# Stacked queries and keys of the first head: transfers issued ahead of the spatial gating, with the weights' priority

## The chip, the cores and the metric

The kernel runs on one core of one Trainium2 chip. The metric is device time in microseconds (us), one launch for the whole computation. The time before is 2175.99 us, the median of three runs (2171.11, 2175.99, 2178.37).

## The reference, cut to what matters

The program is one hybrid layer (dilated attention beside a gated linear recurrence, width 1024, 512 tokens) followed by two layers of a second kind on the same 512 tokens, which also read a context of 256 tokens. The change lies in the second kind alone. One such layer, shortened:

```
zc = split(modulate(rms(h_ctx)) @ w_in[l], 10)      # 256 context tokens
zx = split(modulate(rms(x)) @ w_in[l], 10)          # 512 tokens
k1, k2 = concat(context keys, token keys)           # 768 keys for the tokens
y_a = conformer_conv(a_val, a_gate)                 # 31 taps
p1 = softmax(q1 k1^T * s); p2 = softmax(q2 k2^T * s)
y_b = rms((p1 - lam * p2) @ v)                      # 4 heads, 32 + 32 wide queries, 64 wide values
y_c = gelu(u) * (w_s @ layer_norm(gelu(v)))         # spatial gating
y_d = bg * depthwise_conv(cg * xin)                 # short convolution
x = x + gate * concat(y_a, y_b, y_c, y_d) @ w_out
x = x + gate2 * relu(modulate(rms(x)) @ w1)^2 @ w2
if l == 0: the same mixer and channel mixer on the context, which attends to its own 256 keys
```

## The kernel before, in words

Everything is held transposed, channels on the 128 partitions and tokens along the row. Every float32 operand of a matmul is kept as a rounded high part and a low part (`split`, L188), and a product is three matmuls (`mm3`, L156: high by high L157, high weights by low activations L158, low weights by high activations L159; `tok3` L164 to L166 for outputs that have tokens on the partitions).

**Weights.** A weight block comes as two halves of 128x1024. `raw_half` (L132) issues one 512 KB transfer on SyncE's queue (SP) into the tile `raw`, which has four buffers, under a priority raised by `HP` = 4000. `whalf` (L144) casts it to `whi` on ScalarE (L149) and takes the rest, `wlo`, on VectorE (L150); that last step frees the raw buffer, and the next transfer waits for it. `whi` and `wlo` have three buffers each.

**Order.** The code is traced in program order and a scheduler draws up the order of each engine's instructions ahead of the run: of the instructions that are ready by its own reckoning it takes the one of the best priority, which is the place in program order, moved forward under `tc.high_priority(offset=HP)` and back under `bg(...)`. On the chip each engine, and SP's queue of transfers too, then goes through its list strictly in that order, and an instruction that has to wait holds up what stands behind it.

**The mixer.** `Mixer` holds one stream: the context `sc` (256 tokens, layer 0 only, `mc`) or the tokens `sx` (`mx`). Its parts are `conv` (gated input, then 31 taps on VectorE, L872, most of them in the background), `qkv`, `spatial`, `short`, `attention`, `conv_norm` and `out_part`. The sequence is: `mc.conv`, `mc.qkv`, `mc.spatial`, `mc.short`, `mc.attention`; then per layer `mx.conv`, `mx.qkv`, in layer 0 `mc.conv_norm` and `mc.out_part` (with the context rows `xc` read back from memory, L1215, and stored, L1217), then `mx.spatial` and `mx.attention`, within which `short` and `out_part` of the tokens are run in the background.

**Stacking.** `qkv` leaves queries and keys as [128, 2, n] tiles (two heads of 2 x 32 channels on the partitions, high and low part). For the scores, `load_head` copies each head's 32 rows into a [96, 2, n] tile three times, queries as high, low, high (`qst`) and keys as high, high, low (`kst`), so that one matmul over 96 rows makes the three products of `mm3`. These are transfers from SBUF to SBUF on SP (L1034), 32 partitions each: per head of the context 6 of queries and 6 of keys, per head of the tokens 6 of queries and 12 of keys (two key sources). Both tiles have `ST_BUFS` = 2 buffers, so two heads are in flight. The pool `stk` that they come from opens after `hc`, which holds the rotary table `rope`, is closed, and before the pools of the spatial gating.

**Attention.** One unit is a head and 128 queries: scores `sc` (L1057), maximum (L1061), exponentials (L1065), the difference of the two softmaxes, transposes (L1081), the product with v (L1084). The scores of the next unit are traced ahead of the current unit's rest. For the tokens the scores take three banks of PSUM in the pool `ps_d`, which is opened after the pool that the spatial gating used is closed, so they lie on banks that the gating has to leave first (its last reader there is L951 on VectorE, `sb`).

Of the kernel before, what the change touches and what calls it, by code (L numbers as in the profile page):

```python
# [10 lines left out]
F32 = mybir.dt.float32  # L11
F32R = mybir.dt.float32r
# [67 lines left out]
def tile_net(ctx: ExitStack, tc: tile.TileContext, wst, vec, crow, lrow, sgw, cst, xT, xN, cT, out):  # L80
    nc = tc.nc
    V, A, G, T = nc.vector, nc.scalar, nc.gpsimd, nc.tensor
    HP = 4000
    uid = [0]

    def nm(s):
        uid[0] += 1
        return f"{s}_{uid[0]}"

    def open_pool(name, side="left", space=None, bufs=1):  # L90
        kw = {} if space is None else {"space": space}
        g = tc.tile_pool(name=name, bufs=bufs, side=side, reuse_waits="tile", **kw)
        return g, g.__enter__()
# [104 lines left out]
    class Sums:  # L198


        def __init__(self, n, acc=None, bank=None):
            self.n, self.acc, self.bank, self.parts = n, acc, bank or (lambda: ps.mm()), [] if acc is None else [acc]
# [185 lines left out]
    for mp in range(4):  # L388
        u = yap.tile([P, 2, SX], F32, tag="ya", name=nm("u"), bufs=4)
        for i in range(2):  # L390
            m = 2 * mp + i
            dst, src = u[:, i].rearrange("p (i r) -> p r i", r=4), pu[m].rearrange("p (r i) -> p r i", r=4)
# [297 lines left out]
    sx, sc = S(), S()  # L690
# [117 lines left out]
    class Mixer:  # L808


        def __init__(self, l, s, kv, mix, y_tile):
            self.l, self.s, self.kv, self.mix, self.y_tile = l, s, kv, mix, y_tile
            self.y = {}

        def tt(self, name, full=False):
            t = self.mix.tile([P, self.s.n + 4], F32, tag="t", name=nm(name), bufs=TA_BUFS)
# [196 lines left out]
                self.y["a", m] = a  # L1013


        def attention(self, k, bp, stp_, keys, between):
            s = self.s
            nkeys = sum(q.n for q in keys)
            kts = [(q, i) for q in keys for i in range(q.nt)]
            nk = len(kts)  # L1020
            ng = 2 * s.nt

            class Head:
                pass

            def load_head(h):
                hd = Head()
                hd.h = h
                hd.q = stp_.tile([96, 2, s.n], F32R, tag="qst", name=nm("qst"), bufs=ST_BUFS)
                hd.k = stp_.tile([96, 2, nkeys], F32R, tag="kst", name=nm("kst"), bufs=ST_BUFS)  # L1030

                def stack(dst, src, blk, rows):
                    for i, hl in enumerate(rows):
                        nc.sync.dma_start(dst[32 * i:32 * i + 32].bitcast(F32),  # L1034
                                          src[32 * blk:32 * blk + 32, hl].bitcast(F32))

                for w in range(2):
                    blk = 2 * (h % 2) + w
                    stack(hd.q[:, w], s.q[h // 2], blk, (0, 1, 0))
                    o = 0  # L1040
                    for q in keys:
                        stack(hd.k[:, w, o:o + q.n], q.k[h // 2], blk, (0, 0, 1))
                        o += q.n
                return hd

            def weights(hd, qt):

                sm = const.tile([P, 8], F32, tag="sm2", name=nm("sm"), bufs=8)
                if nkeys > 512:
                    st = ps.tile([P, 3, 512], F32, "sc3", nm("sc3")).rearrange("p a b -> p (a b)")  # L1050
                else:
                    st = ps.mm("sc")
                for w in range(2):
                    o = w * nkeys
                    while o < (w + 1) * nkeys:
                        e = min((w + 1) * nkeys, (o // 512 + 1) * 512)
                        T.matmul(st[:, o:e], hd.q[:, w, qt * P:(qt + 1) * P], hd.k[:, w, o - w * nkeys:e - w * nkeys],  # L1057
                                 start=True, stop=True, skip_group_check=True)
                        o = e
                s3 = st[:, :2 * nkeys].rearrange("p (w k) -> p w k", w=2)  # L1060
                V.tensor_reduce(sm[:, 0:2], s3, axis=AX.X, op=ALU.max, negate=True)  # L1061
                pw = []
                for w in range(2):
                    p = bp.tile([P, nkeys], F32, tag=f"p{w}", name=nm("p"), bufs=P_BUFS)
                    A.activation(p, s3[:, w], AF.Exp, bias=sm[:, w:w + 1], accum_out=sm[:, 4 + w:5 + w])  # L1065
                    pw.append(p)
                return pw, sm

            def apply(hd, qt, pw, sm):

                h = hd.h
                V.reciprocal(sm[:, 6:7], sm[:, 5:6])
                V.scalar_tensor_tensor(sm[:, 7:8], sm[:, 6:7], sm[:, 4:5], k.nlam, op0=ALU.mult, op1=ALU.mult)
                V.scalar_tensor_tensor(pw[0], pw[1], sm[:, 7:8], pw[0], op0=ALU.mult, op1=ALU.add)
                V.reciprocal(hd.r1[:, qt, h % 2:h % 2 + 1], sm[:, 4:5])
                pth = bp.tile([P, nkeys], F32, tag="pth", name=nm("pth"), bufs=PT_BUFS)
                for t0 in range(0, nkeys, 512):
                    tn = min(512, nkeys - t0)
                    pt = ps.mm()
                    for i in range(tn // P):  # L1080
                        T.transpose(pt[:, i * P:(i + 1) * P], pw[0][:, t0 + i * P:t0 + (i + 1) * P], ident)  # L1081
                    A.copy(pth[:, t0:t0 + tn], pt[:, :tn])
                for i, (ss, kt) in enumerate(kts):
                    T.matmul(hd.po[:, qt, h % 2], pth[:, i * P:(i + 1) * P], ss.v[:, kt, h],  # L1084
                             start=i == 0 and qt == 0 and h % 2 == 0, stop=i == nk - 1 and qt == s.nt - 1 and h % 2 == 1,
                             skip_group_check=True)

            def heads_norm(o, r1):

                of = o.rearrange("p t h d -> p (t h) d")  # L1090
                rf = r1.rearrange("p t h -> p (t h)")
                sq = bp.tile([P, ng, 64], F32, tag="osq", name=nm("osq"), bufs=1)
                A.activation(sq, of, AF.Square)
                ms = const.tile([P, 16], F32, tag="ms", name=nm("ms"), bufs=3)
                m2 = const.tile([P, 16], F32, tag="ms2", name=nm("ms2"), bufs=2)
                V.tensor_reduce(ms[:, :ng], sq, axis=AX.X, op=ALU.add)
                V.tensor_mul(m2[:, :ng], rf, rf)
                V.tensor_mul(ms[:, :ng], ms[:, :ng], m2[:, :ng])
                V.tensor_scalar(ms[:, :ng], ms[:, :ng], 1.0 / 64.0, EPS, op0=ALU.mult, op1=ALU.add)
                rs = rstd_small(ms[:, :ng], ng)  # L1100
                V.tensor_mul(m2[:, :ng], rs[:, :ng], rf)
                V.tensor_mul(sq, of, m2[:, :ng].unsqueeze(2).broadcast_to([P, ng, 64]))
                pq = ps.mm()
                s2 = sq.rearrange("p (t h) d -> p t (h d)", h=2)
                for i in range(s.nt):
                    T.transpose(pq[:, i * P:(i + 1) * P], s2[:, i], ident)
                a = self.y_tile("b")
                split(a, pq[:, :s.n], k.subg)
                self.y["b", len([q for q in self.y if q[0] == "b"])] = a

            heads = {0: load_head(0)}
            units = [(h, qt) for h in range(4) for qt in range(s.nt)]
            nxt = weights(heads[0], 0)
            for un, (h, qt) in enumerate(units):
                hd = heads[h]
                if qt == 0:
                    if h < 3:
                        heads[h + 1] = load_head(h + 1)
                    if h % 2 == 0:
                        po = ps.mm("po")[:, :ng * 64].rearrange("p (t h d) -> p t h d", h=2, d=64)  # L1120
                        r1 = const.tile([P, s.nt, 2], F32, tag="r1", name=nm("r1"), bufs=2)
                    hd.r1 = r1
                    hd.po = po
                cur = nxt
                if un + 1 < len(units):
                    h2, qt2 = units[un + 1]
                    nxt = weights(heads[h2], qt2)
                apply(hd, qt, *cur)
                if un in between:
                    between[un]()  # L1130
                if self.taps[0] < 31:
                    self.conv_taps(k, self.taps[0] + CONV_STEP)
                if qt == s.nt - 1 and h % 2:
                    heads_norm(po, r1)
# [8 lines left out]
        def out_part(self, names, done=None, bank=None):  # L1143
# [3 lines left out]
            for half in range(2):  # L1147
                w = {n: whalf((key, 2 + half), "ab".index(n), 512) for n in names if n in "ab"}
                for pair in range(2):
                    if "c" in names:  # L1150
                        w["cd"] = whalf((key, half), pair, 256)
                    for i in range(2):
# [7 lines left out]
                        for e, ((hi, lo), kk, mi, a) in enumerate(seq):  # L1160
# [8 lines left out]
                                                         name=nm("y"), bufs=4 if name in "cd" else 8))  # L1169
# [19 lines left out]
    for l in range(2):  # L1189
# [9 lines left out]
        mx = Mixer(l, sx, [sx] if l == 0 else [sx, sc], mix, y_tile)  # L1199
# [20 lines left out]
        g_st, stk = open_pool("stk")  # L1220
        g_y, yp = open_pool("yp", side="right")
        g_s, sgp = open_pool("sgp", side="right")
        mx.spatial(kx, sgp)
        close_pool(g_s)
        ps.close()
# [120 lines left out]
ST_BUFS = 2  # L1346
# [158 lines left out]
```

## Time and profile before

| | |
|---|---|
| median of three runs | 2175.99 us |
| profiled execution | 2175.18 us, span 2173.3 us |
| TensorE busy | 94% of the span, 11020 matmuls |
| VectorE, ScalarE, GpSimd busy | 66%, 37%, 1% |
| DMA | 37.6% of 16 engines, 259.47 MB, 119 GB/s |
| mean granted TensorE clock | 0.978 of full |

The profile is one execution. Its span is the time from the first to the last instruction seen by the profiler; the 1.9 us between it and the execution's own time lie around it. A busy TensorE is not one at its peak, since the ends of matmuls are modelled. "Idle before, releaser" names the event that came last before an instruction began; "issue" there means that the profile shows no event for it.

### The profile page before, as it was taken

The numbers are of one execution on the slowest core, as the hardware profiler recorded it, in microseconds if no ns is written. First come the engines' busy times: TensorE is split into PE (matmuls) and PEld (weight loads), VectorE is DVE, ScalarE is ACT, GpSimd is POOL, SyncE is SP. The second block draws the span as 40 slices with busy tenths as digits, with TensorE's granted clock in tenths as the row PEclk, the third lists the DMA queues.
The fourth block names the chain that finished last, engine by engine and source line by source line (L and its number), as shares of the span: only waits on it lengthen the run. The fifth ranks groups of instructions, "written<-read, shape, count | busy, mean of one in ns | idle before, by whom it ended". The sixth has DMA issues, their size and how long they took to land.

```text
span 2173.3 us, 28000 instructions
## 1 busy us (share of the span) xinstructions
PE 2053.4 (94%) x11020; PEld 1758.3 (81%) x11020; DVE 1424.4 (66%) x2351; ACT 810.1 (37%) x1266; POOL 27.4 (1%) x28
## 2 busy tenths in 40 slices
PE   7989999999999988998999999999998998999997
PEld 5778788778889777876888888888887787888886
DVE  8778999843458999778354645534798766443444
ACT  3565333432344533645312313123434544232331
POOL 0000000000000000000000000000000000000000
PEclk9999999999999999998999999999999998999998
DMA  8523666523335444222232454422413212333331
GB/s 314 171 92 95 197 222 204 181 94 105 109 111 168 124 121 127 78 78 79 67 127 88 138 169 150 155 67 89 135 59 107 83 59 69 97 97 97 97 97 58
DMA packets 84388, 259.47 MB, mean 119 GB/s; under 512 B 11424, under 2 KB 20256, under 8 KB 84256
## 3 DMA queue, kind: packets, MB, share of 16 engines
q1 hardware_dynamic: 84256, 257.67, 37.6%
q8 instruction: 87, 1.43, 0.3%
q14 instruction: 45, 0.37, 0.1%
HBM read 242.95 MB, written 5.24 MB: 114 GB/s over the span
## 4 chain that ended last, share of the span: by engine, by line
PE 72%; DVE 18%; DMA 3%; issue 3%; ACT 3%; POOL 1%; SPq 0%; POOLq 0%; DVEq 0%; ACTq 0%
PE mm L157 15%; PE mm L159 15%; PE mm L158 15%; PE g L157 5%; PE g L158 5%; PE g L159 5%; DVE wlo L150 3%; DVE ya L872 2%; PE po L1084 2%; DVE rawa L263 2%; DVE j L263 1%; PE sc L1057 1%; DMA rawa<-wst 1%; PE mm L1081 1%; PE mm L208 1%
## 5 line engine op out<-in xcount | busy, mean ns | idle before, releaser
L149 ACT CAST whi<-raw 128x1024 fp32r<-128x1024 f32 x312 | 326.9, 1050 | 536.7 <-PE mm L158 387.4
L150 DVE TENSOR_TENSOR wlo<-raw,whi 128x1024 fp32r<-128x1024 f32 x312 | 380.5, 1222 | 210.7 <-ACT whi L149 205.9
L157 PE MATMUL mm<-h,whi 128*128 128x512 f32 (+1 forms) x992 | 361.0, 366 | 5.7 <-ACT h L338 3.6
L158 PE MATMUL mm<-h,whi 128*128 128x512 f32 (+1 forms) x992 | 361.7, 365 | 0.9 <-DVE h L712 0.9
L159 PE MATMUL mm<-h,wlo 128*128 128x512 f32 (+1 forms) x992 | 361.1, 364 | 0.8 <-DVE wlo L150 0.8
L159 PE MATMUL mm<-hid,wlo 128*128 128x512 f32 (+1 forms) x768 | 272.6, 355 | 1.0 <-DVE wlo L150 1.0
L157 PE MATMUL mm<-hid,whi 128*128 128x512 f32 (+1 forms) x768 | 273.0, 355 | 0.0
L158 PE MATMUL mm<-hid,whi 128*128 128x512 f32 (+1 forms) x768 | 272.8, 355 | 0.0
L157 PEld LDWEIGHTS mm<-h,whi 128*128 128x128 f32 x992 | 188.8, 191 | 37.1 <-ACT h L338 4.0
L158 PEld LDWEIGHTS mm<-h,whi 128*128 128x128 f32 x992 | 188.7, 190 | 31.5 <-DVE h L712 1.9
L157 PE MATMUL g<-h,whi 128*128 128x512 f32 x512 | 205.7, 402 | 8.6 <-DVE v L508 6.0
L159 PEld LDWEIGHTS mm<-h,wlo 128*128 128x128 f32 x992 | 188.6, 190 | 31.2 <-DVE wlo L150 2.0
L158 PE MATMUL g<-h,whi 128*128 128x512 f32 x512 | 204.8, 400 | 0.0
L159 PE MATMUL g<-h,wlo 128*128 128x512 f32 x512 | 204.3, 399 | 0.3 <-DVE wlo L150 0.3
L159 PEld LDWEIGHTS mm<-hid,wlo 128*128 128x128 f32 x768 | 146.1, 190 | 21.5 <-DVE wlo L150 1.4
L157 PEld LDWEIGHTS mm<-hid,whi 128*128 128x128 f32 x768 | 146.4, 191 | 20.2
L158 PEld LDWEIGHTS mm<-hid,whi 128*128 128x128 f32 x768 | 146.3, 191 | 20.0
L1284 DVE SCALAR_TENSOR_TENSOR r<-mm,r 128x512 f32<-128x512 f32 x96 | 57.4, 599 | 114.1 <-ACT r L1283 114.0
L157 PEld LDWEIGHTS g<-h,whi 128*128 128x128 f32 x512 | 98.4, 192 | 26.9 <-issue 6.2
L159 PEld LDWEIGHTS g<-h,wlo 128*128 128x128 f32 x512 | 98.1, 192 | 19.3 <-DVE wlo L150 0.7
L158 PEld LDWEIGHTS g<-h,whi 128*128 128x128 f32 x512 | 98.3, 192 | 17.9
L872 DVE SCALAR_TENSOR_TENSOR ya<-glu,caw,ya 128x512 f32<-128x512 f32 (+1 forms) x180 | 111.6, 656 | 0.5
(309 smaller groups left out, 3462.7 us busy)
## 6 DMA issues: line engine op xcount, KB each, us to landing
raw<-wst SPq DMA_DIRECT2D x312, 512.0 KB, 3.9
rawa<-wst SPq DMA_DIRECT2D x120, 512.0 KB, 4.6
qst<-q SPq DMA_DIRECT2D x48, 64.0 KB, 2.0
kst<-k SPq DMA_DIRECT2D x48, 64.0 KB, 2.0
kst<-k SPq DMA_DIRECT2D x72, 32.0 KB, 2.1
x<-xT SPq DMA_DIRECT2D x4, 512.0 KB, 5.0
hs_d<-c SPq DMA_DIRECT2D x4, 512.0 KB, 2.6
hq<-hs_d SPq DMA_DIRECT2D x4, 512.0 KB, 5.5
```

Of the source, the lines that this page charges most:

```text
L149: A.copy(hi, src)
L150: V.tensor_sub(lo, src, hi.bitcast(F32))
L157: T.matmul(ps, lh, rh, start=start, stop=False)
L158: T.matmul(ps, lh, rl, start=False, stop=False)
L159: T.matmul(ps, ll, rh, start=False, stop=stop)
L208: T.matmul(pt[:, i:i + 1], a[:, i * P:(i + 1) * P], ones1, start=k == 0 and i == 0, stop=k == len(self.parts) - 1 and i == nt - 1, skip_gr ...
L263: V.tensor_tensor_reduce(o, w, row, 0.5, 0.0, ALU.mult, ALU.add, d)
L872: V.scalar_tensor_tensor(self.ya[m], x, w, self.ya[m], op0=ALU.mult, op1=ALU.add)
L1057: T.matmul(st[:, o:e], hd.q[:, w, qt * P:(qt + 1) * P], hd.k[:, w, o - w * nkeys:e - w * nkeys], start=True, stop=True, skip_group_check=True)
L1081: T.transpose(pt[:, i * P:(i + 1) * P], pw[0][:, t0 + i * P:t0 + (i + 1) * P], ident)
L1084: T.matmul(hd.po[:, qt, h % 2], pth[:, i * P:(i + 1) * P], ss.v[:, kt, h], start=i == 0 and qt == 0 and h % 2 == 0, stop=i == nk - 1 and q ...
L1284: V.scalar_tensor_tensor(r, p, 0.0, r, op0=ALU.max, op1=ALU.mult)
```

## The change

`load_head` becomes a method of `Mixer`, without changes to the tiles that it allocates. Three things differ. In the token mixers of both layers, head 0 is loaded right after the pools are opened and before `spatial` is traced, and `attention` takes that head from `mx.first` (the context mixer has none and loads head 0 in `attention` as before). Every transfer of every head of all three attentions is issued under the priority that weights have (`HP`). And within a head the keys go first, then the queries.

```
@@ class Mixer
-            self.y = {}
+            self.y, self.first = {}, None
...
+        def load_head(self, h, stp_, keys):
+            s, hd = self.s, S()
+            hd.h = h
+            hd.q = stp_.tile([96, 2, s.n], F32R, tag="qst", name=nm("qst"), bufs=ST_BUFS)
+            hd.k = stp_.tile([96, 2, sum(q.n for q in keys)], F32R, tag="kst", name=nm("kst"), bufs=ST_BUFS)
+
+            def stack(dst, src, blk, rows):
+                for i, hl in enumerate(rows):
+                    with tc.high_priority(offset=HP):
+                        nc.sync.dma_start(dst[32 * i:32 * i + 32].bitcast(F32),
+                                          src[32 * blk:32 * blk + 32, hl].bitcast(F32))
+
+            for w in range(2):
+                blk, o = 2 * (h % 2) + w, 0
+                for q in keys:
+                    stack(hd.k[:, w, o:o + q.n], q.k[h // 2], blk, (0, 0, 1))
+                    o += q.n
+                stack(hd.q[:, w], s.q[h // 2], blk, (0, 1, 0))
+            return hd
@@ attention
-                        nc.sync.dma_start(dst[32 * i:32 * i + 32].bitcast(F32),
-                                          src[32 * blk:32 * blk + 32, hl].bitcast(F32))
-                for w in range(2):
-                    blk = 2 * (h % 2) + w
-                    stack(hd.q[:, w], s.q[h // 2], blk, (0, 1, 0))
-                    o = 0
-                    for q in keys:
-                        stack(hd.k[:, w, o:o + q.n], q.k[h // 2], blk, (0, 0, 1))
-                        o += q.n
...
-            heads = {0: load_head(0)}
+            heads = {0: self.first or self.load_head(0, stp_, keys)}
...
-                        heads[h + 1] = load_head(h + 1)
+                        heads[h + 1] = self.load_head(h + 1, stp_, keys)
@@ layers
         g_s, sgp = open_pool("sgp", side="right")
+        mx.first = mx.load_head(0, stk, [sx, sc])
         mx.spatial(kx, sgp)
```

## Rows read from the trace of the kernel before

**Rows 1.** The page: engine busy us; DMA issues with KB each, us to landing.

```profile
PE 2053.4 (94%) x11020; PEld 1758.3 (81%) x11020; DVE 1424.4 (66%) x2351; ACT 810.1 (37%) x1266; POOL 27.4 (1%) x28
...
raw<-wst SPq DMA_DIRECT2D x312, 512.0 KB, 3.9
...
kst<-k SPq DMA_DIRECT2D x48, 64.0 KB, 2.0
```

**Rows 2.** Stretches: length, then busy PE, PEld, DVE, ACT, POOL, PEclk, DMA, GB/s.

```profile
700.00:760.00 60.00, 56.20 (x347) 48.46 (x347) 53.99 (x138) 30.41 (x70) 1.80 (x2) 0.99 0.45 132
...
842.00:860.00 18.00, 13.12 (x64) 10.60 (x64) 17.24 (x35) 6.85 (x10) 1.39 (x2) 0.94 0.04 15
860.00:920.00 60.00, 60.00 (x342) 50.37 (x341) 46.78 (x75) 35.43 (x70) 1.01 (x1) 0.96 0.33 95
...
1656.00:1662.00 6.00, 0.64 (x4) 0.47 (x3) 5.89 (x10) 1.36 (x3) 0.00 (x0) 0.83 0.29 76
1662.00:1667.00 5.00, 5.00 (x14) 3.96 (x14) 4.88 (x9) 0.70 (x2) 0.00 (x0) 0.52 0.68 185
```

**Rows 3.** TensorE's waits, 685 to 770 us: total, times, longest.

```profile
PE sc L1057 <- DMA kst<-k: 3.1, 2, 2.1
```

**Rows 4.** Context attention, SP, DVE, ACT in time: start, duration, engine, what.

```profile
702.90 1.86 SPq L1034 DMA_DIRECT2D qst<-q  x3
...
707.43 1.20 DVE L150 TENSOR_TENSOR wlo<-raw,whi 128x1024 fp32r<-128x1024 f32 x1
...
708.67 1.81 SPq L140 DMA_DIRECT2D raw<-wst  x2
...
714.87 1.47 SPq L140 DMA_DIRECT2D raw<-wst  x2
716.39 1.15 SPq L1034 DMA_DIRECT2D kst<-k  x2
...
717.75 1.05 ACT L149 CAST whi<-raw 128x1024 fp32r<-128x1024 f32 x1 [0.27 <-PE g L158]
```

**Rows 5.** Chain that ended last, 710 to 724 us: one piece.

```profile
716.39 5.39 DMA kst<-k
```

**Rows 6.** Layer 0, SP's queue after the rotary table is free.

```profile
792.68 1.78 SPq L1034 DMA_DIRECT2D qst<-q  x3
794.50 3.76 SPq L1034 DMA_DIRECT2D kst<-k  x6
798.30 0.59 SPq L1034 DMA_DIRECT2D qst<-q  x1
798.94 1.55 SPq L1215 DMA_DIRECT2D xc<-cT  x3
...
839.80 1.77 SPq L1034 DMA_DIRECT2D kst<-k  x3
```

**Rows 7.** Layer 0, context rows' first addition, its fifth matmul group, the gating's last matmuls.

```profile
805.02 0.48 DVE L1139 SCALAR_TENSOR_TENSOR xc<-g,der,xc 128x256 f32<-128x256 f32 x1
...
813.95 0.58 PE L159 MATMUL g<-y,wlo 128*128 128x256 f32 x1 [0.90 <-DVE wlo L150]
...
858.39 0.55 PE L157 MATMUL mm<-sgs,sv 128*128 128x256 f32 x1 [3.91 <-DVE sb L951]
```

**Rows 8.** Layer 1, head 0's transfers, the gating's last reads, first scores.

```profile
1632.37 4.07 SPq L1034 DMA_DIRECT2D qst<-q  x3
...
1643.39 3.76 SPq L1034 DMA_DIRECT2D kst<-k  x6
...
1659.53 1.97 DVE L951 SCALAR_TENSOR_TENSOR sb<-mm,vecs,lrow 64x256 f32<-64x256 f32 x4
...
1661.60 1.62 PE L1057 MATMUL sc<-kst,qst 96*128 96x512 f32 x4 [5.36 <-issue]
```

**Rows 9.** Layer 0, token attention: one weight transfer, and its cast.

```profile
882.85 0.34 SPq L140 DMA_DIRECT2D raw<-wst  x1
...
923.62 1.05 ACT L149 CAST whi<-raw 128x1024 fp32r<-128x1024 f32 x1 [0.95 <-PE g L158]
```

More of the change, by code (lines that the diff above doesn't have):

```diff
@@ L1021, in attention @@
             ng = 2 * s.nt
[L1023 to L1033, printed above, removed]
-                        nc.sync.dma_start(dst[32 * i:32 * i + 32].bitcast(F32),
-                                          src[32 * blk:32 * blk + 32, hl].bitcast(F32))
-                for w in range(2):
-                    blk = 2 * (h % 2) + w
-                    stack(hd.q[:, w], s.q[h // 2], blk, (0, 1, 0))
-                    o = 0
-                    for q in keys:
-                        stack(hd.k[:, w, o:o + q.n], q.k[h // 2], blk, (0, 0, 1))
-                        o += q.n
-                return hd
             def weights(hd, qt):
```

## The prediction, made before the changed kernel ran

> **What bounds the kernel now.** I read the page first, then the busy time by stretches, the waits and the chain around the three attentions, and last SP's queue in order of time. TensorE is busy 2053.4 of 2173.3 us [rows 1], so only a gap on TensorE can be won, and the change can win one only where TensorE waits for a stacking transfer, directly or through the order of its instructions. The reader is to see three places. (a) The context attention, 700 to 760 us: TensorE is busy 56.20 of 60 us [rows 2] and two of its gaps, 3.1 us in all, end on a key transfer [rows 3]; these are the only waits for stacking that TensorE has. (b) The start of the token attention in layer 0: TensorE is idle there because the gating's last matmuls wait 3.91 us for VectorE [rows 7], which is busy 17.24 of 18 us [rows 2]. (c) The same start in layer 1: TensorE is idle 5.36 us before the first scores, and the profile names no releaser [rows 8]. Within the token attention TensorE is busy 60.00 of 60 us [rows 2].
>
> **The first head of the tokens, moved ahead.** In layer 1 the transfers of head 0 are issued from 1632.37 on, and the last six key transfers end on SP at 1643.39 + 3.76 = 1647.15 us [rows 8]; with the 2.0 us to landing that the page has for a key transfer [rows 1] head 0 is complete at about 1649. The first scores start at 1661.60. Here 12.5 us of slack lie between. What ends last there is the gating's last reads of PSUM by VectorE, 1659.53 + 1.97 = 1661.50, a tenth of a microsecond before the scores [rows 8], and the three banks of the scores lie where the gating's were. So an earlier head 0 gives 0 here. In layer 0 head 0 goes out from 792.68 and even head 1's last transfers are issued by 839.80 + 1.77 = 841.6 [rows 6], while the gating still holds TensorE at 858.39 [rows 7]: 15 us of slack for two heads, again 0. Both ends of this term: 0, and the whole gap of 5.36 if the unnamed wait is a transfer after all (a rival below).
>
> The row shows the transfers complete well before the wait ends. The Trainium skill (DMA: Bandwidth & Descriptors, section Rules for kernel authors) advises to issue a DMA early, compute, and wait on its semaphore late, so that its fixed cost overlaps. By that rule alone moving head 0 ahead would be worth the 5.36 us; by the row the overlap is there already, and I go by the row.
>
> The keys before the queries: both parts of head 0 are needed before its second score group, so the order within a head gives nothing by itself; 0.
>
> **The priority, context attention.** This is where I expect a gain. SP issues three query transfers at 702.90, then weights at 708.67 and 714.87, and the two key transfers at 716.39 stand right behind two weights of 512 KB each [rows 4]; the key transfer takes 5.39 us until it has landed [rows 5] against a median of 2.0 [rows 1]. TensorE waits for it. With the weights' priority, and traced before the token mixer's weights, the stacking goes in front of these, and both gaps close: -3.1 us [rows 3].
>
> What it pushes back: a stacking transfer costs SP 3.76/6 = 0.63 us [rows 6], head 0 of the context has 12 of them, 7.6 us, and heads 0 and 1 together 15.1 us. Begun at 702.90, they end at 710.5 or at 718.0. The weight transfer of 708.67 (freed by the split that ends at 707.43 + 1.20 = 708.63) is the fourth after it, with four raw buffers, so it is cast at 717.75 [rows 4]. It lands at about 708.67 + 3.9 [rows 1] = 712.6 and has 5.2 us of slack. Pushed to 710.5 it costs 0; pushed to 718.0, 9.3 later, it costs 9.3 - 5.2 = 4.1 us at the first matmuls of the token mixer. Ends 0 and 4.1; I take 0, because the raw transfers keep the same priority as the stacking and only those of later program order stand back.
>
> **The priority, layer 0's context output.** At 792.68 the rotary table is free and stacking starts; after ten transfers come the context rows `xc`, which have no raised priority but stand earlier in the program [rows 6]. Now the 18 + 18 - 10 = 26 transfers left of heads 0 and 1 may go first: 26 x 0.63 = 16.4 us, `xc` at 815.3, landed, with the weights' 3.9 us as a bound for these smaller loads [rows 1], at 819.2. The first addition, at 805.02 before, then ends at about 819.7; the output has four banks, and the fifth group's matmuls, at 813.95 before [rows 7], wait for it: 5.7 us. Of this the 3.91 us that TensorE waits for VectorE at the end of the gating [rows 7] can be given back, since VectorE fills the time with taps that it would run there. So this term lies between 0 (the ten and the rest stay spread as now) and 5.7; I take 5.7 - 3.9 = 1.8.
>
> **Elsewhere.** Heads 2 and 3 of the tokens now pass weights that run `short` and `out_part` in the background: 18 x 0.63 = 11.3 us on SP per head. A weight transfer at 882.85, issued as its buffer came free, is cast at 923.62, four buffers on [rows 9], 40 us, so 11.3 us of delay are hidden; 0. Heads 2 and 3 also wait for a buffer that the scores free, and a weight behind such a wait is held up, by the same slack at no cost. Work on TensorE, VectorE and ScalarE is the same, instruction for instruction, and the number of transfers too.
>
> **Sum.** 2175.18 - 3.1 + 0 + 1.8 = 2173.9, say 2174 us. The profiled execution stands 0.8 us under the median of the runs, which I leave inside the rounding.
>
> **Rivals.**
>
> Faster: the unnamed wait of 5.36 us in layer 1 is for head 0 (or the planner, believing head 0 late, orders around it). Then that gap goes, and with it the slow clock after it: from 1662 to 1667 the granted clock is 0.52, the lower of the two levels, after TensorE had been nearly idle for 6 us [rows 2], and 5.0 us of matmuls would take 2.6, 2.4 us less. 2175.2 - 3.1 - 5.4 - 2.4 = 2164. For it: the profile names no releaser, which is how a wait that was over long before looks as well as one that it can't see. Against it: the 0.1 us between VectorE's last read and the scores.
>
> Slower: a solid block of stacking transfers on the one queue holds up what stands behind it, from the point where more than about 20 of them go before the first `xc` or before the token mixer's first weight. Price: 5.7 + 4.1 us, of which nothing is given back, and the gain of 3.1 goes, since TensorE waits for the weight in the same place: 2175.2 + 9.8 = 2185. For it: SP's queue is strictly in order and the 36 transfers of two heads take 22.7 us of it, as long as that stretch. Against it: the stacking of one head has to wait for its sources and buffers, which leaves room for others.
>
> The rows show a key transfer behind two weights landing late. The Trainium skill (the same page, section Queues, rings and completion order) says that on each of the 16 DMA engines descriptors are taken in the ring's order. The trace agrees with its 5.39 us; by it, priority only swaps who waits, which is this rival's case and not the forecast's.
>
> Nothing moves: queries come from the split that `qkv` does last, the pool from the table that this frees, so the transfers can't start sooner, and the context's gaps close only to be refilled by VectorE, which is busy 53.99 of 60 us there [rows 2]. Time 2175.
>
> **Chances.** Forecast 0.34, nothing moves 0.15, faster 0.28, slower 0.23. What a measurement of this kernel can tell from no change is about 0.3%, 6.5 us; the forecast and the case in which nothing moves lie within it. So faster 0.28, same 0.49, slower 0.23. The range takes in both rivals' times, 2163 to 2185.5, since each holds more than 2 in 10; the forecast's own range is 2169 to 2180, which is the sum with 5.4 us won and with 5.7 us lost. The order of instructions is drawn up anew for the whole program, which I can't price and which the outer range has to hold.
>
> **What would show it.** In the changed profile TensorE's waits for a key transfer in the context attention should be gone (3.1 us before); the scores in layer 1 should still start a tenth of a microsecond after L951's last read; in layer 0 the `xc` loads should come later than ten transfers after the table is free, and the first L1139 with them. The forecast is wrong if the 5.36 us gap closes while L951 stays where it is, if the fifth output group waits more than 4 us, or if the granted clock or the busy time of an engine differs in stretches without attention.

## The result, and the profile after

The changed kernel takes 2195.1 us (median of four runs, 2191.85 to 2196.76) against 2175.09 us for the kernel before (four runs): a ratio of 1.0091 with a 95% interval of 1.0069 to 1.0113, slower by 20 us. The profiled execution took 2196.27 us, its span is 2194.4 us.

The page after, busy time and the two issues that [rows 1] show:

```profile
PE 2057.2 (94%) x11020; PEld 1762.5 (80%) x11020; DVE 1426.3 (65%) x2351; ACT 809.2 (37%) x1266; POOL 28.1 (1%) x28
...
raw<-wst SPq DMA_DIRECT2D x312, 512.0 KB, 3.8
...
kst<-k SPq DMA_DIRECT2D x48, 64.0 KB, 2.0
```

Work and counts are what they were, and landing times too, within 0.1 us. The span is 21.1 us longer and TensorE's busy time 3.8 us, so the rest is idle time of TensorE. To find where, I cut both traces at seven events of TensorE that both have, and at the end (E): the matmul after the wait for q of the context (A), the token mixer's first matmul (X), the mean of the context's norm (S), the first matmul of the context's output (B), the first of the gating (G), the first token scores in layer 0 (C) and in layer 1 (D). The lengths, taken from the starts in the timeline, in us:

```
                 A-X   X-S   S-B   B-G   G-C    C-D    D-E
before          24.4  68.3   9.0  30.6  32.7  801.8  511.7
after           24.5  71.2   9.3  47.8  33.1  802.1  511.8
```

Of 21.3 us, 17.2 lie in the context's output (B to G), 2.9 in the context attention and the token mixer's projections (X to S), 0.4 in the gating and the rest within 0.3. TensorE's waits there, first 685 to 770 us (compare [rows 3]):

```profile
PE g L157 <- ACT whi L149: 3.6, 1, 3.6
```

and 770 to 880 us (total, times, longest):

```profile
PE g L157 <- DVE xc L1137: 18.9, 1, 18.9
PE mm L157 <- DVE sb L951: 5.8, 2, 5.2
```

The waits for keys of [rows 3] are gone, and 3.6 us for a weight's cast stand in their place. The timelines of SP, ScalarE and TensorE have the reason: 24 stacking transfers go out before the next two weights, and the cast waits for a weight to land.

```profile
704.28 1.87 SPq L1026 DMA_DIRECT2D kst<-k  x3
...
719.72 0.59 SPq L1026 DMA_DIRECT2D kst<-k  x1
720.41 1.00 SPq L140 DMA_DIRECT2D raw<-wst  x2
...
724.86 1.04 ACT L149 CAST whi<-raw 128x1024 fp32r<-128x1024 f32 x1 [2.76 <-DMA raw<-wst]
...
725.95 0.79 PE L157 MATMUL g<-h,whi 128*128 128x512 f32 x1 [3.63 <-ACT whi L149]
```

By these waits alone X to S would be 0.5 us longer (3.6 against 3.1). The other 2.4 us are TensorE's busy time, 66.82 us against 64.46 for the same work. Behind the 3.63 us wait its granted clock is 0.50 (1.2 GHz) from 725.9 to 731.0 us; in the kernel before, the mean of the whole stretch is 1.00. X to S before, then after, then the 5.1 us behind the wait (columns as in [rows 2]):

```profile
719.29:787.55 68.26, 64.46 (x356) 53.93 (x355) 63.02 (x146) 29.56 (x69) 2.42 (x2) 1.00 0.33 99
719.17:790.36 71.19, 66.82 (x354) 55.73 (x353) 62.70 (x144) 30.27 (x70) 2.21 (x2) 0.95 0.37 117
725.90:731.00 5.10, 5.05 (x14) 4.18 (x15) 3.90 (x9) 2.34 (x8) 0.00 (x0) 0.50 0.22 50
```

The 18.9 us are new: the fifth matmul group of the context's output finds no free bank, since the additions of the context rows (L1137, formerly L1139) have not been done. Why they were late is seen on SP's list (L1026 stacking, L1213 `xc`, L140 weights), the answer to [rows 6]:

```profile
793.43 1.15 SPq L1026 DMA_DIRECT2D kst<-k  x2
795.85 0.51 SPq L1026 DMA_DIRECT2D qst<-q  x1
796.40 0.59 SPq L1026 DMA_DIRECT2D kst<-k  x1
797.03 0.59 SPq L1026 DMA_DIRECT2D qst<-q  x1
797.67 5.02 SPq L1026 DMA_DIRECT2D kst<-k  x8
806.92 0.33 SPq L140 DMA_DIRECT2D raw<-wst  x1
807.30 0.51 SPq L1026 DMA_DIRECT2D kst<-k  x1
...
811.08 2.21 SPq L1026 DMA_DIRECT2D kst<-k  x3
815.18 2.60 SPq L140 DMA_DIRECT2D raw<-wst  x3
...
827.95 0.59 SPq L1026 DMA_DIRECT2D kst<-k  x1
828.59 2.03 SPq L1213 DMA_DIRECT2D xc<-cT  x4
```

The `xc` loads, formerly at 798.94 behind ten stacking transfers, are issued at 828.59 behind all 36. The 36 take 35.1 us, 793.43 to 828.54. Their own issue, 0.61 each, is 22 us of it. Of the other 13, 4.2 us are one weight's wait for its buffer (802.69 to 806.92), 1.9 another's (813.29 to 815.18), 1.3 the wait for the rotary table (794.58 to 795.85), and the rest is shorter waits and the issue of the weights: weights of the context's output keep their place in program order between the stacking, and on a strict list what they wait for, everything behind them waits for. The chain from there:

```profile
817.43 15.24 DVE ya L872 x23
832.66 0.41 DVE xc L1137
833.07 0.14 issue
833.21 0.55 PE g L157
```

VectorE fills the time with taps of the convolution; `xc` lands, the first addition ends at 833.06 and TensorE goes on, after 18.87 us. Two things end together here: the loads land 3.7 to 4.2 us after their issue, and VectorE's list has 23 taps ahead of the first addition, which end at 832.66. In e2, e5 and e6 below, VectorE waits another 0.2 to 0.7 us for the transfer after the same 23 taps, so there the transfer ends last; what the taps alone would have cost was not tried. In the kernel before, the first matmul of the same group started after a short wait for a cast:

```profile
812.31 0.39 PE L157 MATMUL g<-y,whi 128*128 128x256 f32 x1 [1.51 <-ACT whi L149]
```

At the gating's end nothing is given back: the wait for L951, 3.91 us before [rows 7], is 5.19 us now. In layer 1, from VectorE and TensorE's timeline, all is as in [rows 8]:

```profile
1680.53 1.97 DVE L951 SCALAR_TENSOR_TENSOR sb<-mm,vecs,lrow 64x256 f32<-64x256 f32 x4
...
1682.60 0.77 PE L1055 MATMUL sc<-kst,qst 96*128 96x512 f32 x1 [5.36 <-issue]
```

### The profile page after: what moved, and what is told of

Same layout as the page of the kernel before. It is cut to its first block, busy times and chain, and to the rows that moved or that the text cites. A ratio compares the mean times of both kernels' runs of the same rounds, so it can differ in the third digit from the quotient of the medians.

```text
span 2194.4 us, 27974 instructions
## 1 busy us (share of the span) xinstructions
PE 2057.2 (94%) x11020; PEld 1762.5 (80%) x11020; DVE 1426.3 (65%) x2351; ACT 809.2 (37%) x1266; POOL 28.1 (1%) x28
## 4 chain that ended last, share of the span: by engine, by line
PE 75%; DVE 16%; ACT 3%; DMA 3%; issue 2%; POOL 1%; SPq 0%; POOLq 0%; DVEq 0%; ACTq 0%
PE mm L157 16%; PE mm L159 16%; PE mm L158 16%; PE g L157 5%; PE g L159 5%; PE g L158 5%; DVE wlo L150 3%; DVE ya L872 3%; PE po L1082 2%; DVE rawa L263 2%; DMA rawa<-wst 1%; PE sc L1055 1%; PE g L165 1%; PE g L166 1%; DVE j L263 1%
## 5 line engine op out<-in xcount | busy, mean ns | idle before, releaser
L1297 DVE SCALAR_TENSOR_TENSOR x<-mm,der,x 128x512 f32<-128x512 f32 x64 | 48.0, 750 | 96.5 <-PE mm L159 96.5
```

What stands on the lines that cost most here:

```text
L1297: V.scalar_tensor_tensor(s.x[m], p, s.mod[:, 40 + m:41 + m], s.x[m], op0=ALU.mult, op1=ALU.add)
```

## The experiments

The theory after the result: the four `xc` loads, which have no raised priority, now stand behind 36 stacking transfers on SP, and this costs some 17 us; the raised priority in the context attention costs some 3 more by pushing back an early weight of the token mixer; moving head 0 does nothing. Each experiment is an edit to the changed kernel unless it says "kernel before". Their stage lengths stand together after the last one.

**The priority taken back (e1), and the priority alone (e2).**

```
e1:  -                    with tc.high_priority(offset=HP):
     +                    with tc.high_priority(offset=0):
e2:  -        mx.first = mx.load_head(0, stk, [sx, sc])
```

> The changed kernel with the stacking transfers' priority taken back; head 0 is still loaded ahead of the gating and keys still go before queries. On SP's list the four xc loads then stand after ten stacking transfers again, as before the change. Theory (the loads of the context rows, pushed behind all 36 stacking transfers of two heads, cost the 18.9 us gap in layer 0's context output, and the raised priority in the context attention some 3 us): the gap is gone, time 2173 to 2178 us, the same as before. Rival (loading head 0 ahead of the gating is what costs): about 2195 us.

> The changed kernel without the earlier load of head 0; only the priority and the order of keys and queries are changed. SP's list is the same as the changed kernel's, entry by entry. Theory: 2194 to 2196 us, the gap of 18.9 us as in the changed kernel, since moving head 0 in the program does nothing once its transfers have the priority. Rival (moving head 0 ahead costs part of it): under 2190 us.

e1: 2177.18 us, ratio 1.0006 (0.9992 to 1.0020). e2: 2193.97 us, 1.0080 (1.0055 to 1.0105). The loss comes with the priority and goes with it; loading head 0 ahead of the gating, and keys before queries, change nothing that can be measured.

**The context rows raised too (e3).**

```
+                with tc.high_priority(offset=HP):
                     nc.sync.dma_start(t, cT[:, m:m + 2])
```

> The changed kernel, and the four loads of the context rows xc in layer 0 get the weights' priority too; on SP's list they then stand after ten stacking transfers instead of 36. Theory: the wait of TensorE for the first additions goes from 18.9 us to under 2 us and the time to 2176 to 2180 us (some 3 us of the loss lie earlier, in the context attention). Rival (the block of stacking transfers holds up the weights of the context output, and xc is only what ends last): TensorE then waits for whi or wlo in the same place, at least 8 us of the gap stay, 2186 us or more.

2180.34 us, 1.0019 (1.0006 to 1.0033), 0.3 us over the time expected. TensorE's waits from 800 to 850 us in it:

```profile
PE g L159 <- DVE wlo L150: 1.5, 2, 0.9
PE g L157 <- ACT whi L149: 1.5, 1, 1.5
PE g L165 <- DVE wlo L150: 0.8, 1, 0.8
```

No wait for `xc` is left, and B to G is 30.7 us again. Some 4 us of the loss stay.

**The mirror image: the kernel before, with xc alone put back (e6).**

```
+                with bg(800):
                     nc.sync.dma_start(t, cT[:, m:m + 2])
```

> The kernel before, with one edit: the four xc loads of layer 0 get a lower priority, so that on SP's list they stand after all 36 stacking transfers; no stacking transfer has its priority raised and no order within a head is changed. Theory: this alone brings the gap of some 17 to 19 us at the fifth output group and 2190 to 2195 us. Rival (the block of raised stacking transfers does the harm in another way, through weights or through the order on VectorE): the additions come late but the time stays under 2185 us.

2191.05 us, 1.0068 (1.0044 to 1.0092), and from 790 to 850 us:

```profile
PE g L157 <- DVE xc L1139: 19.2, 1, 19.2
```

With no stacking transfer raised, the late `xc` by itself makes the gap. e3 and e6 together settle the cause of the large part.

**Which attention's priority (e4, e5, e12).**

```
e4:  HP if s is sc else 0                    (and no early head 0)
e5:  HP if s is sx and self.l == 0 else 0
e12: as e5, and the xc loads raised as in e3
```

> Priority raised in the context attention alone, keys first everywhere, head 0 not moved. Theory: the token mixers' first matmuls wait some 3.6 us for a cast instead of 3.1 us for keys, the stretch up to the rotary table ends about 3 us later than before, no gap at the context output: 2176 to 2180 us. Rival (all of the loss comes from the context attention, by way of the order that follows from it): 2190 us or more.

> The changed kernel with the raised priority in layer 0's token attention alone; the context attention and layer 1 have it taken back. On SP's list the four xc loads stand after all 36 stacking transfers, as in the changed kernel, while the start of the list, with the context attention, has weights and stacking mixed as before. Theory (two losses that add up: some 17 us by xc, some 4 us in the context attention): the gap of 18 to 19 us at the context output is there, the cast's wait of 3.5 us at the token mixer's first weight is not, 2190 to 2193 us against 2194 with both. Rival (the late xc needs the context attention's shift too): under 2185 us.

> The changed kernel with the raised priority in layer 0's token attention alone (none in the context attention, none in layer 1), and the four xc loads of layer 0 raised too. Both losses that the theory names are taken away at once: the gap at the context output under 2 us, no cast's wait at the token mixer's first weight, 2173 to 2179 us, no difference from the kernel before that can be measured. Rival (a third loss sits in the block of raised stacking transfers itself): 2182 us or more.

e4: 2181.45 us, 1.0023 (1.0004 to 1.0042), 1.5 us over its expectation. e5: 2194.44 us, 1.0079 (1.0055 to 1.0103), 1.4 us over its own. So the tokens' priority carries the large loss. The context's, raised alone, carries a small one, just clear of noise; beside the large loss it can't be seen in the time, since e2 with both has 1.0080 and e5 without it 1.0079. In e4 TensorE's waits, 685 to 770 us, are those of the changed kernel with the cast in the place of the keys:

```profile
PE g L157 <- DVE q L195: 3.9, 1, 3.9
PE g L157 <- ACT whi L149: 3.4, 1, 3.4
```

e12 missed: 2181.31 us, 1.0023 (1.0013 to 1.0034), where I expected no difference. Its gap at `xc` and its cast's wait are gone as expected, but G to C, the gating, takes 36.2 us in it and in e3, 3.5 more than before; in the trace, TensorE's list has the gating's four groups of token products all behind the projection, and waits for VectorE three times before them (840 to 870 us):

```profile
PE mm L157 <- DVE sb L951: 4.4, 3, 2.1
PE mm L157 <- ACT sv L933: 1.9, 1, 1.9
```

Both kernels that have this raise `xc` and the tokens' stacking together; which of the two orders TensorE's list so was not tried. The rival of e12, a third loss, is right for 3.5 us in the two kernels where `xc` is raised; the changed kernel itself has 33.1 us there. Half of the 3.5 us is TensorE's busy time at a lower mean clock (28.7 us at 0.88 in both, 26.95 at 0.97 before).

**Stacking on another queue (e8 kernel before, e11 changed kernel).**

```
-                        nc.sync.dma_start(dst[32 * i:32 * i + 32].bitcast(F32),
+                        nc.gpsimd.dma_start(dst[32 * i:32 * i + 32].bitcast(F32),
```

> The kernel before, with all stacking transfers issued by GpSimd instead of SP, so that no transfer of SP's list stands behind a stacking transfer or the other way round. Theory: the two waits of TensorE for keys in the context attention (3.1 us), which come from transfers behind 512 KB weights on SP's list, shrink or go; the rest is as before; 2170 to 2177 us. Rival (the key transfers land late because the DMA engines are busy with weights, whichever queue issued them): the waits for keys stay at 3 us or grow and the time is 2176 us or more.

> The changed kernel, head 0 ahead, priority and all, with one edit: the stacking transfers are issued by GpSimd and not by SP. Theory (the priority does harm only because stacking, xc and weights share SP's one list in strict order): neither the gap of 18.9 us at the context output nor the wait of 3.6 us for the cast of the token mixer's first weight is left, and the waits for keys in the context attention are gone too: 2170 to 2176 us. Rival (stacking sent early takes the DMA engines from weights and xc, whichever list it stands on): at least 8 us of the loss stay, 2183 us or more.

e8: 2173.91 us, 0.9988 (0.9975 to 1.0002). The key waits are gone, with no raised priority, but it gives 3.6 us back between C and D. e11: 2200.3 us, 1.0109 (1.0094 to 1.0123), against both the theory, which had 2170 to 2176, and the reason that its rival gave. GpSimd's timeline in it:

```profile
796.89 1.97 POOL L1026 DMA_DIRECT2D qst<-q  x4
...
800.31 2.94 POOL L1026 DMA_DIRECT2D kst<-k  x6
...
805.69 1.48 POOL L1026 DMA_DIRECT2D kst<-k  x3
807.16 0.50 POOL L1026 DMA_DIRECT2D qst<-q  x1
807.67 6.66 POOL L225 TENSOR_TENSOR rs<-ms,neghalf 128x2 f32<-128x2 f32 x1
```

and its TensorE:

```profile
814.72 0.69 PE L241 MATMUL g<-ident,rb 128*128 128x128 f32 x2 [24.94 <-DVE rb L238]
```

The two harms named are gone, and the same one has come back on the other list: the power (L225) of the context's norm, whose input VectorE wrote at 789.81, has no raised priority and stands behind 34 raised stacking transfers on GpSimd. It starts at 807.67, after the last transfer of the block at 807.16, and takes 6.66 us; the same shape takes 0.70 at 856.38 in that trace. S to B is 32.3 us, 23.3 more. On SP the `xc` loads go out at 785.59 there, and nothing waits for them. So the harm isn't SP's alone, and it isn't that of the DMA engines: on both lists tried it is a block of transfers with raised priority ahead of work that has none.

**The unnamed wait of layer 1 (e10, kernel before).**

```
-            pr = ps.mm()
+            pr = ps.g() if l else ps.mm()
...
-                    pg = ps.mm()
+                    pg = ps.mm("sc" if l == 0 and s is sx else "mm")
```

> The kernel before, with the gating's PSUM moved: in layer 0 its token products use the two idle score banks of the context attention, and in layer 1 the bias product is put on a g bank, so that the g banks come first in that pool and the token scores no longer lie on the gating's mm banks. No transfer is touched. Theory (the unnamed 5.36 us wait before layer 1's first scores is for VectorE's last reads of the gating's banks, L951, not for head 0's transfers): the scores start before the last L951 ends, the gap shrinks to under 3.5 us, and the 3.9 us wait in layer 0 shrinks; 2165 to 2173 us. Rival (head 0's transfers end that wait): the 5.36 us gap stays, 2172 us or more.

2176.43 us, 1.0004 (0.9991 to 1.0018). The timeline of TensorE and VectorE in layer 1:

```profile
1655.48 0.87 PE L1057 MATMUL sc<-kst,qst 96*128 96x512 f32 x4
...
1658.69 1.99 DVE L951 SCALAR_TENSOR_TENSOR sb<-mm,vecs,lrow 64x256 f32<-64x256 f32 x4
1659.81 0.76 PE L157 MATMUL g<-h,whi 128*128 128x512 f32 x1 [3.00 <-DVE sb L951]
...
1666.30 0.80 PE L159 MATMUL g<-h,wlo 128*128 128x512 f32 x1 [4.29 <-DVE wlo L150]
```

With the banks apart and the transfers untouched the scores run at 1655.48, 3 us before the last reads of the gating begin, without a wait: head 0, whose last key transfers leave SP by 1646.79 there and by 1647.15 before, was there, and the 5.36 us were the wait for L951. The time is not won, because the next matmuls wait 3.00 and 4.29 us for VectorE in the same place, and layer 0 gets a wait of 5.75 us before its scores for the 3.9 it had. The expected gain of the kernel as a whole missed; the mechanism held.

**Another queue for the context's stacking alone (e13, kernel before).**

```
-                        nc.sync.dma_start(dst[32 * i:32 * i + 32].bitcast(F32),
+                        (nc.gpsimd if s is sc else nc.sync).dma_start(dst[32 * i:32 * i + 32].bitcast(F32),
```

> The kernel before, with the context attention's stacking transfers issued by GpSimd and the tokens' by SP as before; no priority is raised. Theory (what the raised priority was to win, the keys' wait in the context attention, is won without its price where the transfers leave the list that weights and xc are on, as in the run with all stacking on GpSimd, which gained 3.3 us up to the context's norm and 1.6 us in its output and gave back 3.6 us from the tokens' scores on): 2169 to 2173 us, no wait of TensorE for keys over 1 us in the context attention. Rival (what was given back there has nothing to do with GpSimd's transfers for the tokens): 2174 us or more.

2171.66 us, 0.9987 (0.9976 to 0.9998). TensorE's waits, 700 to 800 us:

```profile
PE g L208 <- ACT sq L217: 4.3, 2, 3.4
PE g L241 <- DVE rb L238: 1.7, 1, 1.7
PE sc L1057 <- ACT p L1065: 1.2, 1, 1.2
```

No wait for keys and none for a cast. The gain is some 3 us; the interval allows 0.4 to 5.

Stage lengths of all, in us, one profiled execution each:

```
                 X-S   S-B   B-G   G-C    C-D    D-E
e1 no priority  70.5   9.0  31.6  32.7  802.7  511.8
e2 only prio    70.6   9.3  48.0  33.1  801.3  511.7
e3 xc raised    69.7   9.3  30.7  36.2  801.8  511.7
e4 context      70.7   9.3  31.0  32.7  804.2  513.4
e5 tokens       69.2   9.0  48.4  33.1  802.1  511.7
e6 xc late      67.5   9.0  48.6  33.1  802.1  512.1
e8 pool         65.0   9.1  29.0  32.7  805.4  512.6
e10 banks       68.7   9.0  31.6  32.8  797.0  517.5
e11 changed,pool 66.2 32.3  28.3  33.1  803.6  513.1
e12 tokens,xc   69.2   9.0  30.6  36.2  801.5  512.1
e13 ctx pool    65.2   9.1  29.0  32.4  803.1  512.0
```

B to G is 28 to 32 us wherever `xc` goes out early and 48 wherever it goes out late, without exception. X to S moves by 1 to 2 us between kernels with the same edit there, so a few tenths in it mean nothing: the four with the context raised have 69.7 to 71.2, the six others on SP's list 67.5 to 70.5. The clock takes part in this: its mean from X to S is 0.95 in the changed kernel, e2 and e4 and 0.98 in e3, against 1.00 in four of the six others and 0.98 in e1 and e12.

## Why the prediction was wrong, point by point

- **Head 0 ahead: 0.** Right. e2, without it, is as slow as the changed kernel; e1, with it, is as fast as the kernel before. The rule of issuing early (the Trainium skill, DMA: Bandwidth & Descriptors, section Rules for kernel authors) gives nothing where the row shows the transfer landed 12.5 us ahead. The slack that [rows 8] give was real, as e10 shows.
- **The unnamed wait is VectorE's.** Right, shown by e10. With it the faster rival, which I gave 0.28, falls.
- **Context attention, -3.1 us, with 0 to 4.1 given back.** The waits for keys went as forecast. I took the lower bound of what is given back; it was nearly the upper: SP goes from 704.28 to 720.31 with 24 stacking transfers and no weight, two weights follow at 720.41, and the cast of the token mixer's weight is at 724.86 instead of 717.75. TensorE waits 3.63 us there. The sum also had no term for the clock behind this wait, which goes with the 2.4 us of busy time shown above (5.1 us at half the clock are worth some 2.5 us, an estimate from the row of 725.90 to 731.00). So X to S came out 2.9 us longer where 3.1 were to be won: this step failed too, by 6.0 of the 21 us. The reason that I gave for the lower bound, that weights of earlier program order keep their place, is true and doesn't bear on this weight, which comes later in the program than both heads.
- **Layer 0's context output, 0 to 5.7, taken as 1.8.** This is the step that failed by most, 15.4 of the 21 us by which the forecast fell short. Its mechanism was the right one, `xc` behind 26 more transfers and the fifth group without a bank, and its size was not: 17.2 us from B to G, with a gap of 18.87. Two parts of the working are to blame. I took 16.4 us for the 26 transfers from their issue time alone and had `xc` at 815.3; it came at 828.59, 13.3 later. The table came free some 3 us later than before (795.77 against 792.61), and weights stand between the stacking with their waits for buffers, which hold up the whole list. The gap is 18.87 against 5.7, 13.2 more. That these two differences agree is luck: 813.95 in [rows 7] is the fifth matmul of the fifth group, whose first starts at 812.31, 1.51 us of waiting included, while in the changed kernel all of this runs some 3 us later and the gap begins at 814.34; the two errors cancel. And I let 3.91 us be given back at the gating; that wait grew to 5.19.
- **The slower rival** named this place and this mechanism and put it at 2185, with 0.23. Its price had the same fault, so the range, which ends at 2185.5, ends 10 us short of the time. What the prediction took for it from the Trainium skill (DMA: Bandwidth & Descriptors, section Queues, rings and completion order), that each DMA engine takes descriptors in its ring's order, is not what decided: what came late was issued late, by SP (828.59) or GpSimd (807.67), in an order drawn up before the run.
- **Rows against the range.** The prediction had a row that would have warned: [rows 4] have weights and stacking alternating on SP, and between their entries lies time that no issue fills: in that trace SP's last stacking transfer before the weight of 708.67 (704.87, 0.52 us long) ends at 705.39, and the 3.3 us between are the weight's wait for the split that frees its buffer at 708.63. Reading such a stretch by its length, not by the sum of its entries, would have raised the price; whether to the 35.1 us measured, no row of the kernel before says.

## What to carry to other kernels

Raising the priority of transfers on a queue that others share puts back everything on it that isn't raised; list what stands there, loads that some engine needs within the next few microseconds first, and ask for each when it would go out. Price the delay from the measured length of such a stretch of the queue, waits included, since a strict list passes on the waits of its entries and not only their issue time. Where a few transfers do wait in vain, another queue for these alone (e13) beats a better place on the old one, but only if that queue has no urgent work either (e11).

## What the runs showed of the hardware

- A stacking transfer from SBUF to SBUF costs SP some 0.6 us to issue. By the page of the kernel before, a key transfer of 64 KB lands in 2.0 us and one of 32 KB in 2.1 (medians). One of 32 KB right behind two weights of 512 KB took 5.39 us [rows 5]; the prediction set it against the median of the 64 KB ones, which changes little. On GpSimd's list the issue is 0.50 us (e11).
- A power of [128, 2] on GpSimd took 6.66 us right behind a block of 34 transfers that GpSimd had issued, and 0.70 us when nothing stood ahead of it (e11, L225). Behind three such transfers (e8, at 792.63) it took 1.02. What makes up the 6 us was not tried. The Trainium skill (GPSIMD Engine Reference, section When to use GPSIMD) says that the descriptors of a DMA that GpSimd issues are generated by GpSimd's own cores; that would fit, and no run here shows it.
- After its 18.87 us of idle time TensorE's clock was at the lower of its levels for some 5 us: the granted clock is 0.50 (1.2 GHz) from 833 to 838 us and 1.00 (2.4 GHz) from 838 to 842:

```profile
833.00:838.00 5.00, 4.79 (x22) 4.83 (x23) 4.55 (x9) 0.00 (x0) 0.00 (x0) 0.50 0.43 152
838.00:842.00 4.00, 3.73 (x32) 3.52 (x30) 3.55 (x6) 1.05 (x1) 0.00 (x0) 1.00 0.09 33
```

The columns are the stretch, its length, busy time of TensorE, its weight loads, VectorE, ScalarE and GpSimd, the granted clock, DMA share and GB/s: 22 matmuls took 4.79 us there, and 32 took 3.73 behind it.
